# Fixed byte offsets for the moving operands of a decoder step: H at 96 and L at 0 modulo 256

## The chip, the cores and the metric

The kernel runs on one NeuronCore of one Trainium2 chip. The metric is the device time of one execution in microseconds (us), lower is better; several executions are timed and the median is quoted. A profile of one execution gives, for each engine, when each instruction began and how long it was busy. The engines are PE (matrix multiply, with PEld as its weight loads), DVE (elementwise, vector), ACT (activation functions), POOL (GpSimd) and SP (which only issues DMAs here).

## The reference, cut to what matters

One inference step of a two-layer hybrid decoder, for 256 prompt positions and 8 sampled positions (264 columns together), model width 2048, float32. Layer 0 is dilated sliding-window attention and layer 1 an S5 state-space layer with a gated output; each is followed by a gated MLP with a causal convolution of width 3.

```
for i in range(DEPTH):
    hp = rms_norm(xp, norm_g[i, 0])
    ...
    xp = xp + rms_norm(mp, norm_g[i, 1])
    hp = rms_norm(xp, norm_g[i, 2])
    fp, cp = conv_ffn(hp, c0_p, w_up[i], conv_w[i], conv_b[i], w_down[i])
    xp = xp + rms_norm(fp, norm_g[i, 3])
```

The work is almost all in eight dense products with float32 weights: `w_qkv`, `w_o`, `w_up`, `w_down` of layer 0, `w_in`, `w_glu`, `w_up`, `w_down` of layer 1.

## The kernel before, in words

Activations lie transposed: 128 channels on the partitions, the 264 positions along the free dimension. To reach float32 accuracy with the faster float32r matmul, each operand is split in two parts that are rounded in turn: a high part H (ACT writes it) and the rest L (DVE writes it). A product is then three matmuls into one PSUM tile: weights-H with activations-H (line 202), weights-H with activations-L (line 203), weights-L with activations-H (line 204). The activations are the moving operand (264 columns), the 128x128 weight block is the stationary one, loaded anew for every matmul.

`gemm` (line 180) walks an order of (k, m) pairs, k a block of 128 input channels and m one of 128 output channels. Each order begins with a group of 4 to 6 output blocks that are done together, k outermost (`order_grouped`, line 67): there one moving operand pair serves several products one after the other. After it, one output block at a time runs through all k: there each product has another operand pair. There are 6176 products, so 18528 of these matmuls. Of the products, 16x5 in `w_qkv`, 8x5 in `w_o`, 16x6 in each `w_up`, 16x4 in `w_in` and 16x5 in `w_glu` stand in the groups, 456 in all; the other 5720 run in the second form.

Weights stream from HBM in tiles of 512 KB by SP; `ensure` and `split` (lines 165 and 161) make their H and L parts, on ACT and DVE, in buffers of 4096 bytes per partition.

Each H, each L, each block of the residual stream and each block of a product's output is a tile of 1056 bytes per partition (264 floats) from the function `act` (line 155). Most come from the pool `acts` of 44 such buffers (line 1213); the pools `o`, `z`, `ga` and `gb` hold more of them for a stage. A pool's buffers lie behind one another, so successive buffers start 1056 = 4 x 256 + 32 bytes apart, and the start of a buffer modulo 256 takes all eight multiples of 32. Which buffer an H or an L gets is a matter of which is free. In the built program the 6176 H operands start at all eight of these offsets, between 198 and 1456 times each, and so do the L operands. All weight parts start at 64 modulo 256 (block columns are 512 bytes apart).

`residual` (line 339) makes, block by block, the sum of stream and normed output, its H and L for the next product (`operand`, line 327) and its store to DRAM. `reload` (line 314) brings the stream back by DMAs that POOL issues, into free `act` buffers, long before `residual` needs it. DMAs issued by POOL use a scratch area for their descriptors, 16 KB per partition by default. The tile framework orders each engine's instructions by its own scheduler and adds the waits.

Of the kernel before, what the change touches and what calls it, by code (L numbers as in the profile page):

```python
# [17 lines left out]
F32 = mybir.dt.float32  # L18
F32R = mybir.dt.float32r
# [7 lines left out]
P = 128  # L27
# [34 lines left out]
GS = 6  # L62
WARM = (6, 8, 9)
POOL_K = (2, 3, 8, 9, 13)


def order_grouped(mts, nk, first):
# [56 lines left out]
class Kern:  # L124
    def __init__(self, ctx, tc, I, O):
        self.ctx, self.tc, self.nc, self.I, self.O = ctx, tc, tc.nc, I, O
        self.n = 0
        self.tick = 0
        self.tasks = []
        self.side = iter(())  # L130
        self.loaded = []

    def nm(self, s):
        self.n += 1
# [17 lines left out]
    def tt(self, out, a, b, op):  # L152
        self.nc.vector.tensor_tensor(out, a, b, op=op)

    def act(self, pool, dt=F32):
        return pool.tile([P, NT], dt, tag="act", name=self.nm("act"))

    def small(self, tag, bufs=2):
        return self.sp.tile([P, NT], F32, tag=tag, name=self.nm(tag), bufs=bufs)
# [142 lines left out]
    def yevac(self, ys, gi):  # L302

        sq = [None, None]

        def f(m, ps):
            y = self.act(self.actp)
            self.squares(sq, ps[:, 0:NT])
            self.nc.vector.tensor_scalar(y, ps[:, 0:NT], self.gain(gi, m), None, op0=ALU.mult)
            ys[m] = y  # L310

        return f, sq

    def reload(self, src, wait):

        xs = []

        def load(k):
            x = self.act(self.actp)
            self.nc.gpsimd.dma_start(x, src[k])  # L320
            xs.append(x)

        for k in range(KD):
            self.later(wait + k // 2, lambda k=k: load(k))
        return xs

    def operand(self, x, gi, k):

        nc = self.nc
        g = self.gain(gi, k)  # L330
        hi, lo = self.act(self.actp, F32R), self.act(self.actp, F32R)
        nc.scalar.activation(hi, x, AF.Copy, scale=g)

        def low():
            nc.vector.scalar_tensor_tensor(lo, x, g, hi.bitcast(F32), op0=ALU.mult, op1=ALU.subtract)  # L335

        return hi, lo, low
# [50 lines left out]
    def consts(self):  # L388
        nc, I = self.nc, self.I
        cp = self.cp  # L390
        self.gn = cp.tile([P, 8 * KD], F32, name="gn")
        nc.scalar.dma_start(self.gn, I["gn"])
        self.ident = cp.tile([P, P], F32, name="ident")
        self.later(2, lambda: nc.gpsimd.dma_start(self.ident, I["ident"]))
        self.onesm = cp.tile([P, 1], F32, name="onesm")
        nc.vector.memset(self.onesm, -0.5 / D)
        self.epsm = cp.tile([P, 1], F32, name="epsm")
        nc.vector.memset(self.epsm, -0.5 * EPS / P)
        self.wm = cp.tile([P, P], F32, name="wm")
        nc.vector.memset(self.wm, 1.0)  # L400
        self.ident15 = cp.tile([TB, TB], F32, name="ident15")
        self.later(6, lambda: nc.scalar.activation(self.ident15, self.ident[0:TB, 0:TB], AF.Copy, scale=1.5))
        self.ones = cp.tile([P, NS], F32, name="ones")
        nc.vector.memset(self.ones, 1.0)
# [279 lines left out]
    def prompt_out(self, ap, st, h, os_):  # L684

        nc = self.nc
        po = self.ps()
        hi, lo = st["o", h] = (self.act(self.bigp, F32R), self.act(self.bigp, F32R))
        st["left", h], st["os"] = 2, os_
        ps = {}  # L690

        def tr(g):

            pt = self.ps()
            for c in range(3):
                nc.tensor.transpose(pt[:, c * P : (c + 1) * P], st["S", g, h][:, c * P : (c + 1) * P], self.ident)
            ps[g] = ap.tile([P, 384], F32, tag="pt", name=self.nm("pt"), bufs=3)
            nc.scalar.activation(ps[g], pt[:, 0:384], AF.Copy)

        def pv(g):  # L700
            vt, p = st["vt", g, h], ps[g]
            nc.tensor.matmul(po[:, 0:256], vt[:, 0:128], p[:, 0:256], start=(g == 0), stop=False)
            nc.tensor.matmul(po[:, 128:256], vt[:, 128:256], p[:, 256:384], start=False, stop=(g == G - 1))
            if g == G - 1:
                self.split(hi[:, 0:NP], lo[:, 0:NP], po[:, 0:NP])
                self.finished(st, h)

        for g in range(G):
            self.later(g, lambda g=g: tr(g))
            self.later(g + 1, lambda g=g: pv(g))  # L710
# [24 lines left out]
    def ffn(self, fp, l, rhs, rget, prep, gi, src, gpool):  # L735
        nc, I, O = self.nc, self.I, self.O
        cw, cst, keep = prep
        gate = {}
        gs = [None] * FT

        def evac(m, ps):
            u = fp.tile([P, NT], F32, tag="U", name=self.nm("U"), bufs=6)
            nc.vector.tensor_tensor(u, ps[:, 0:NT], rget(), op=ALU.mult)  # L743
            nc.gpsimd.tensor_copy(keep[:, m, :], u[:, NP - 2 : NT])  # L744
            c = fp.tile([P, NT], F32, tag="C", name=self.nm("C"), bufs=4)
            nc.scalar.activation(c, u, AF.Identity, bias=cw[:, 3, m : m + 1], scale=cw[:, 2, m : m + 1])  # L746
            self.later(1, lambda: conv(m, u, c))

        def conv(m, u, c):
            for j in (1, 0):  # L750
                s = 2 - j
                nc.vector.scalar_tensor_tensor(  # L752
                    c[:, s:NP], u[:, 0 : NP - s], cw[:, j, m : m + 1], c[:, s:NP], op0=ALU.mult, op1=ALU.add
                )
            nc.vector.tensor_tensor(c[:, NP:NT], c[:, NP:NT], cst[:, m, :], op=ALU.add)  # L755
            if m < FT:
                nc.scalar.activation(c, c, AF.Silu)  # L757
                gate[m] = c
            else:
                self.later(1, lambda: out(m - FT, c))  # L760

        def out(m, c):
            g = gate.pop(m)
            nc.vector.tensor_tensor(g, g, c, op=ALU.mult)  # L764
            hi, lo = self.act(gpool(m), F32R), self.act(gpool(m), F32R)
            nc.scalar.activation(hi, g, AF.Copy)  # L766
            gs[m] = (hi, lo)
            self.later(1, lambda: nc.vector.tensor_tensor(lo, g, hi.bitcast(F32), op=ALU.subtract))

        self.gemm("w_up%d" % l, ORD_UP, KD, rhs, evac, lag=3)  # L770
        xs = self.reload(src, 8)
        self.later(6, lambda: nc.gpsimd.dma_start(O["conv"][l], keep))
        ys = [None] * KD
        f, sq = self.yevac(ys, gi)

        def grhs(k):
            if k == FT - 1 and self.gwait:
                while gs[k] is None or any(True for t in self.tasks if t[0] <= self.tick + 1):
                    self.pump()
                self.gwait = False  # L780
            return self.ready(gs, k)

        self.gwait = True
        self.gemm("w_down%d" % l, ORD_DOWN, FT, grhs, f)
        return ys, xs, sq
# [260 lines left out]
    def s5(self, p, rhs, rget):  # L1046
# [119 lines left out]
        def back(j, up, y):  # L1166
            V.scalar_tensor_tensor(y, up[:, :, 0:YC], dsk[:, j : j + 1], y, op0=ALU.mult, op1=ALU.add)
            z = p.tile([P, NT], F32, tag="z", name=self.nm("z"), bufs=2)
            A.activation(z[:, 0:NP].rearrange("p (c s) -> p s c", s=T4), y[:, :, 8:YC], AF.Gelu_apprx_tanh)
            A.activation(z[:, NP:NT], y[:, 0, 0:8], AF.Gelu_apprx_tanh)  # L1170
            zp = self.bigp if j < 10 else self.actp
            hi, lo = self.act(zp, F32R), self.act(zp, F32R)
            self.split(hi, lo, z)
            zs[j] = (hi, lo)
            if j == KD - 1:
                Q.dma_start(O["ssms"], news)
                Q.dma_start(O["ssmp"], newp)
# [4 lines left out]
    def glu(self, p, zs, gi):  # L1182
# [5 lines left out]
        def evac(m, ps):  # L1188
# [3 lines left out]
            m -= KD  # L1192
            sg = p.tile([P, NT], F32, tag="gsg", name=self.nm("gsg"), bufs=2)
            nc.scalar.activation(sg, ps[:, 0:NT], AF.Sigmoid)
            y = self.act(self.actp)
            nc.vector.tensor_tensor(y, half.pop(m)[:, 0:NT], sg, op=ALU.mult)
            self.squares(sq, y)
            nc.scalar.activation(y, y, AF.Copy, scale=self.gain(gi, m))
# [6 lines left out]
    def run(self):  # L1205
# [4 lines left out]
        self.wp = ent(tc.tile_pool(name="w", bufs=3))  # L1210
        self.sp = ent(tc.tile_pool(name="small", bufs=2))
        self.psp = ent(tc.tile_pool(name="psum", bufs=8, space=PSUM))
        self.actp = ent(tc.tile_pool(name="acts", bufs=44))
        self.stream, self.bases = [], {}
        for n in ("w_qkv", "w_o", "w_up0", "w_down0", "w_in", "w_glu", "w_up1", "w_down1"):
            self.bases[n] = len(self.stream)
# [7 lines left out]
        def ffn_layer(l, rhs, rget, keep, nxt):  # L1224
            with ExitStack() as s:
                fp = pool(s, f"ffn{l}")
                ga = pool(s, f"ga{l}", 2 * GA)
                gb = []
                s2 = ExitStack()
                if l == 0:  # L1230
# [3 lines left out]
                def gpool(m):  # L1234
# [5 lines left out]
                    if not gb:  # L1240
                        for _ in self.side:
                            pass
                        s2.close()
                        gb.append(pool(s, f"gb{l}", 2 * (FT - GA - GS)))
                    return gb[0]

                prep = self.ffn_prep(fp, l)
# [2 lines left out]

        with ExitStack() as s:
            ap = pool(s, "att")
            self.bigp = pool(s, "o", 2 * H)
            rhs, rget = self.first(ap, I["x"])
            setup = self.s5_setup(ap)
            self.later(70, lambda: setattr(self, "side", setup))
# [8 lines left out]
        rhs, rget = ffn_layer(0, rhs, rget, xd[1], 4)  # L1265
        with ExitStack() as s:
            p = pool(s, "s5")
            self.bigp = pool(s, "z", 20)
            zs = self.s5(p, rhs, rget)
            xs = self.reload(xd[1], 8)  # L1270
            ys, sq = self.glu(p, zs, 5)
# [174 lines left out]
```

## Time and profile before

| what | value |
|---|---|
| median of 3 executions | 2534.36 us (2530.38 to 2537.7) |
| profiled execution: own time | 2533.61 us |
| its span, first to last instruction | 2531.8 us |
| PE busy, share of the span | 2465.2 us, 97% |
| DVE, ACT, POOL busy | 1788.3, 1208.4, 853.9 us |
| mean granted TensorE clock, as a share of full speed | 0.989 |
| DMA traffic | 512.12 MB, mean 202 GB/s |

How to read it: the profile lists matmuls with a start and a modelled end. Matmuls are pipelined, so the busy time of one (some 285 ns) covers its neighbours, and what a matmul costs is the distance from its start to the start of the next. The other engines' times are those of single instructions.

### The profile page before, as it was taken

Reading aid. Unit: us, or ns where it says so; the run is one execution under the profiler, and the core shown is the slowest. Engines: PE = TensorE matmul, PEld = TensorE weight load, DVE = VectorE, ACT = ScalarE, POOL = GpSimd, SP = SyncE. Lnnn points to the kernel's source line nnn. Section 1 sums busy time; section 2 is a strip of 40 time slices with the busy share of each in tenths; the row PEclk is TensorE's granted clock in tenths of the full one; section 3 lists DMA queues with packets and bytes.
Section 4 is the critical chain, followed back from the end, with each engine's and each line's share of the span. In section 5 each row is a group of like instructions: output and inputs, shape, how many; then the busy total and the mean of one; then the engine's idle time right before and its main releaser. Section 6 shows DMA issues by size and latency. Waiting matters only on the chain.

```text
span 2531.8 us, 52652 instructions
## 1 busy us (share of the span) xinstructions
PE 2465.2 (97%) x20998; PEld 2437.6 (96%) x20998; DVE 1788.3 (71%) x3002; ACT 1208.4 (48%) x1946; POOL 853.9 (34%) x1153
## 2 busy tenths in 40 slices
PE   8999999999999999999999988999999999999997
PEld 8999999999999999999998988999999999999997
DVE  6788998779888887764446877446877777764444
ACT  5465545556454554443334333444654454443332
POOL 6444448344999980001004564102100000011001
PEclk9999999999999999999999998999999999999998
DMA  7676666665666665565556777555655555566553
GB/s 276 219 258 227 210 221 222 217 222 182 222 214 221 224 211 184 183 205 197 182 183 213 236 233 217 188 183 176 196 179 181 182 180 180 183 205 199 181 182 118
DMA packets 186870, 512.12 MB, mean 202 GB/s; under 512 B 39280, under 2 KB 68992, under 8 KB 186368
## 3 DMA queue, kind: packets, MB, share of 16 engines
q1 hardware_dynamic: 141808, 457.89, 55.4%
q0 software_dynamic: 7968, 26.71, 3.2%
q10 hardware_dynamic: 36848, 24.16, 3.1%
q8 instruction: 164, 2.69, 0.4%
q14 instruction: 82, 0.67, 0.1%
HBM read 469.80 MB, written 38.88 MB: 201 GB/s over the span
## 4 chain that ended last, share of the span: by engine, by line
PE 73%; DVE 11%; issue 4%; DMA 4%; POOL 3%; ACT 3%; ACTq 1%; SPq 0%; DVEq 0%; POOLq 0%
PE ps L204 23%; PE ps L202 23%; PE ps L203 23%; DVE wlo L163 4%; DVE C L752 2%; ACT whi L162 2%; DMA yb<-y 1%; POOL z_room L920 1%; ACTq L953 1%; DMA y<-yb 1%; DVE act L367 1%; DMA ident<-in_ident 1%; DVE act L335 1%; DVE C L755 0%; DVE U L743 0%
## 5 line engine op out<-in xcount | busy, mean ns | idle before, releaser
L202 PE MATMUL ps<-act,whi 128*128 128x264 f32 x6176 | 1771.8, 288 | 10.7 <-ACT whi L162 7.5
L204 PE MATMUL ps<-act,wlo 128*128 128x264 f32 x6176 | 1762.0, 286 | 18.5 <-DVE wlo L163 18.1
L203 PE MATMUL ps<-act,whi 128*128 128x264 f32 x6176 | 1760.7, 285 | 10.0 <-DVE act L335 9.7
L163 DVE TENSOR_TENSOR wlo<-wraw,whi 128x1024 fp32r<-128x1024 f32 (+1 forms) x775 | 978.2, 1263 | 585.3 <-ACT whi L162 584.5
L162 ACT ACTIVATE whi<-wraw 128x1024 fp32r<-128x1024 f32 (+1 forms) x775 | 814.2, 1053 | 894.8 <-PE ps L203 670.5
L204 PEld LDWEIGHTS ps<-act,wlo 128*128 128x128 f32 x6176 | 1168.6, 189 | 23.5 <-DVE wlo L163 23.4
L203 PEld LDWEIGHTS ps<-act,whi 128*128 128x128 f32 x6176 | 1169.0, 189 | 13.7 <-DVE act L335 12.9
L202 PEld LDWEIGHTS ps<-act,whi 128*128 128x128 f32 x6176 | 1165.8, 189 | 16.4 <-ACT whi L162 8.0
L294 POOL TENSOR_TENSOR acc<-acc,sq 128x264 f32<-128x264 f32 x112 | 112.6, 1005 | 669.0 <-ACT sq L300 666.4
L744 POOL COPY ckeep<-U 128x10 f32<-128x10 f32 x172 | 44.8, 261 | 643.7 <-DVE U L743 642.6
L752 DVE SCALAR_TENSOR_TENSOR C<-U,cw,C 128x255 f32<-128x255 f32 (+1 forms) x344 | 197.4, 576 | 0.7 <-ACT C L746 0.7
L746 ACT ACTIVATE C<-U,cw 128x264 f32<-128x264 f32 x172 | 102.3, 597 | 34.8 <-DVE U L743 30.5
L743 DVE TENSOR_TENSOR U<-ps,rstd 128x264 f32<-128x264 f32 x172 | 73.0, 429 | 62.9 <-PE ps L204 62.8
L449 POOL TENSOR_TENSOR qkv<-qkv,cs 32x264 f32<-32x264 f32 x48 | 59.7, 1243 | 123.5 <-DVE sw L443 45.6
L121 POOL TENSOR_TENSOR z_e<-z_pa,z_pb 128x256 f32<-128x256 f32 x64 | 69.1, 1080 | 5.0
L617 ACT ACTIVATE vc<-vc,pk 128x128 f32<-128x128 f32 x192 | 59.5, 390 | 17.2 <-DMA pk<-pd 17.2
L121 POOL TENSOR_TENSOR z_pa<-z_bc,z_tab 128x256 f32<-128x256 f32 x64 | 62.9, 983 | 2.4
L766 ACT ACTIVATE act<-C 128x264 fp32r<-128x264 f32 x86 | 35.5, 413 | 58.7 <-DVE C L764 58.7
L757 ACT ACTIVATE C<-C 128x264 f32<-128x264 f32 x86 | 35.7, 415 | 48.1 <-DVE C L752 44.4
L121 POOL TENSOR_TENSOR z_pb<-z_bc,z_tab 128x256 f32<-128x256 f32 x64 | 56.6, 884 | 0.0
L450 POOL TENSOR_TENSOR sw<-sw,cs 32x264 f32<-32x264 f32 x48 | 51.6, 1075 | 0.0
L668 ACT ACTIVATE S<-S,nmg 128x128 f32<-128x128 f32 (+1 forms) x48 | 21.4, 447 | 61.2 <-DVE nmg L663 61.2
(215 smaller groups left out, 1771.9 us busy)
## 6 DMA issues: line engine op xcount, KB each, us to landing
wraw<-in_w_up SPq DMA_DIRECT2D x344, 512.0 KB, 3.5
wraw<-in_w_down SPq DMA_DIRECT2D x172, 512.0 KB, 3.8
wraw<-in_w_qkv SPq DMA_DIRECT2D x143, 512.0 KB, 4.8
wraw<-in_w_glu SPq DMA_DIRECT2D x64, 512.0 KB, 3.5
wraw<-in_w_in SPq DMA_DIRECT2D x32, 512.0 KB, 3.9
kc<-in_kc SPq DMA_DIRECT2D x24, 512.0 KB, 5.4
vc<-in_vc SPq DMA_DIRECT2D x24, 512.0 KB, 5.9
wraw<-in_w_o SPq DMA_DIRECT2D x16, 512.0 KB, 3.6
```

The costliest lines, as they stand in the source:

```text
L121: return lambda *a, **k: self.tc.keep_in_program_order(getattr(self.eng, name)(*a, **k))
L162: self.nc.scalar.activation(hi, src, AF.Copy)
L163: self.nc.vector.tensor_tensor(lo, src, hi.bitcast(F32), op=ALU.subtract)
L202: nc.tensor.matmul(o, hi[:, c], xh, start=first, stop=False)
L203: nc.tensor.matmul(o, hi[:, c], xl, start=False, stop=False)
L204: nc.tensor.matmul(o, lo[:, c], xh, start=False, stop=last)
L294: nc.gpsimd.tensor_tensor(st[0], st[0], st[1], op=ALU.add)
L449: nc.gpsimd.tensor_tensor(t[0:ROT, :], t[0:ROT, :], self.cs[:, 0, :], op=ALU.mult)
L617: nc.scalar.activation(vcs[g][:, e], vcs[g][:, e], AF.Copy, scale=pk[:, g, e : e + 1])
L743: nc.vector.tensor_tensor(u, ps[:, 0:NT], rget(), op=ALU.mult)
L746: nc.scalar.activation(c, u, AF.Identity, bias=cw[:, 3, m : m + 1], scale=cw[:, 2, m : m + 1])
L752: nc.vector.scalar_tensor_tensor(c[:, s:NP], u[:, 0 : NP - s], cw[:, j, m : m + 1], c[:, s:NP], op0=ALU.mult, op1=ALU.add)
```

## The change

H and L of one operand now share one buffer, a slot of 576 floats = 2304 = 9 x 256 bytes: `pair` returns H at float 280 (1120 bytes, 96 modulo 256) and L at float 0. The pool `acts` has 22 slots in place of 44 buffers, the pools `o`, `ga`, `gb`, `z` half their number. Blocks that are no moving operand go in twos: `share(k)` puts the stream's block k and the output's block k in the two halves of one slot, at bytes 0 and 1152. Small pads in front (`pad`, with a memset of one element each) bring every pool's base to a multiple of 256. The scratch for POOL's DMAs is cut from 16 to 4 KB per partition.

In the built program every H then starts at 96 and every L at 0 modulo 256; and since the pad of the constants' pool lies ahead of the weight buffers, the weight parts move from 64 to 128 modulo 256. Number and shape of matmuls, weight loads and DMAs stay as they are.

```
+SLOT = 576
+HI, LO = 280, 0
...
-    def act(self, pool, dt=F32):
-        return pool.tile([P, NT], dt, tag="act", name=self.nm("act"))
+    def two(self, pool, dt=F32):
+        t = pool.tile([P, SLOT], dt, tag="act", name=self.nm("act"))
+        return t[:, 0:NT], t[:, SLOT // 2 : SLOT // 2 + NT]
+    def share(self, k):
+        if k in self.halves:
+            return self.halves.pop(k)
+        t, self.halves[k] = self.two(self.actp)
+        return t
+    def pair(self, pool):
+        t = pool.tile([P, SLOT], F32R, tag="act", name=self.nm("act"))
+        return t[:, HI : HI + NT], t[:, LO : LO + NT]
+    def pad(self, pool, n):
+        t = pool.tile([P, n], F32, tag="pad", name=self.nm("pad"), bufs=1)
+        self.tc.keep_in_program_order(self.nc.vector.memset(t[:, 0:1], 0.0))
...
-            y = self.act(self.actp)
+            y = self.share(m)
...
-            x = self.act(self.actp)
+            x = self.share(k)
...
-        hi, lo = self.act(self.actp, F32R), self.act(self.actp, F32R)
+        hi, lo = self.pair(self.actp)
...
+        self.pad(cp, 16)
...
-        self.actp = ent(tc.tile_pool(name="acts", bufs=44))
+        self.actp = ent(tc.tile_pool(name="acts", bufs=22))
...
+                self.pad(fp, 8)
+                ga = pool(s, f"ga{l}", GA)
...
-    nc = bacc.Bacc("TRN2", target_bir_lowering=False, num_devices=1)
+    nc = bacc.Bacc("TRN2", target_bir_lowering=False, num_devices=1, dynamic_dma_scratch_size=4096)
```

The change in the slots also moves some instructions. On PE, at the start of the product with `w_up` of layer 0, stood before (`act_7667` is the H of block 0, `act_7668` its L, the six `ps` are the first six output blocks):

```order
L202 MATMUL ps_7698<-act_7667,whi_7519 128x264
L202 MATMUL ps_7702<-act_7667,whi_7519 128x264
L202 MATMUL ps_7706<-act_7667,whi_7519 128x264
L202 MATMUL ps_7710<-act_7667,whi_7519 128x264
L202 MATMUL ps_7714<-act_7667,whi_7519 128x264
L202 MATMUL ps_7718<-act_7667,whi_7519 128x264
L226 MATMUL ps_8161<-epsm,wm 88x1
L203 MATMUL ps_7698<-act_7668,whi_7519 128x264
L204 MATMUL ps_7698<-act_7667,wlo_7520 128x264
L203 MATMUL ps_7702<-act_7668,whi_7519 128x264
```

and now (`act_7633` holds both parts):

```order
L226 MATMUL ps_7661<-act_7633,whi_7485 128x264
L226 MATMUL ps_7665<-act_7633,whi_7485 128x264
L226 MATMUL ps_7669<-act_7633,whi_7485 128x264
L226 MATMUL ps_7673<-act_7633,whi_7485 128x264
L227 MATMUL ps_7661<-act_7633,whi_7485 128x264
L228 MATMUL ps_7661<-act_7633,wlo_7486 128x264
L227 MATMUL ps_7665<-act_7633,whi_7485 128x264
L228 MATMUL ps_7665<-act_7633,wlo_7486 128x264
```

Lines 226, 227, 228 of the changed file are lines 202, 203, 204 of the one before (line 226 of the one before is a one-column matmul of the norm). Four products with H stand ahead of the first with L, where there were six.

On POOL, near the end of the product with `w_qkv`, where the residual stream is brought back for the first sum, stood before:

```order
L600 COPY vn_6939<-qkv_6688 128x8
L320 DMA act_7141<-in_x 128x264
L600 COPY vn_6939<-qkv_6788 128x8
L320 DMA act_7143<-in_x 128x264
L320 DMA act_7148<-in_x 128x264
L320 DMA act_7150<-in_x 128x264
L600 COPY vn_6939<-qkv_6878 128x8
```

and now:

```order
L625 COPY vn_6920<-qkv_6669 128x8
L625 COPY vn_6920<-qkv_6769 128x8
L344 DMA act_7026<-in_x 128x264
L344 DMA act_7028<-in_x 128x264
L344 DMA act_7076<-in_x 128x264
L344 DMA act_7078<-in_x 128x264
L344 DMA act_7112<-in_x 128x264
L344 DMA act_7114<-in_x 128x264
L344 DMA act_7121<-in_x 128x264
L344 DMA act_7123<-in_x 128x264
L344 DMA act_7128<-in_x 128x264
L344 DMA act_7130<-in_x 128x264
L625 COPY vn_6920<-qkv_6859 128x8
```

Ten of the sixteen loads now wait for the end of that product, where four did; the other six stand at its beginning, as twelve did.

## Rows read from the trace of the kernel before

**Rows 1.** The page's first part: busy time, share of the span, instructions.
```profile
span 2531.8 us, 52652 instructions
PE 2465.2 (97%) x20998; PEld 2437.6 (96%) x20998; DVE 1788.3 (71%) x3002; ACT 1208.4 (48%) x1946; POOL 853.9 (34%) x1153
```

**Rows 2.** The page's groups: line engine op out<-in xcount | busy, mean ns | idle before, releaser.
```profile
L202 PE MATMUL ps<-act,whi 128*128 128x264 f32 x6176 | 1771.8, 288 | 10.7 <-ACT whi L162 7.5
L204 PE MATMUL ps<-act,wlo 128*128 128x264 f32 x6176 | 1762.0, 286 | 18.5 <-DVE wlo L163 18.1
L203 PE MATMUL ps<-act,whi 128*128 128x264 f32 x6176 | 1760.7, 285 | 10.0 <-DVE act L335 9.7
```

**Rows 3.** Three stretches: length, busy (count) of PE, PEld, DVE, ACT, POOL; clock; DMA.
```profile
1100.00:1350.00 250.00, 250.00 (x2063) 250.00 (x2062) 117.45 (x117) 98.39 (x107) 25.23 (x38) 1.00 0.59 192
1820.00:2240.00 420.00, 420.00 (x3454) 420.00 (x3453) 300.97 (x505) 210.76 (x288) 13.81 (x72) 1.00 0.57 181
2300.00:2500.00 200.00, 200.00 (x1658) 200.00 (x1657) 90.24 (x82) 77.45 (x82) 13.74 (x13) 1.00 0.56 183
```

**Rows 4.** Timeline of PE: first matmul of successive runs on one operand pair (start, us).
```profile
19.89 0.28 PE L202 MATMUL ps<-act,whi 128*128 128x264 f32 x1
...
21.71 0.28 PE L202 MATMUL ps<-act,whi 128*128 128x264 f32 x1
...
23.54 0.28 PE L202 MATMUL ps<-act,whi 128*128 128x264 f32 x1
...
25.35 0.29 PE L202 MATMUL ps<-act,whi 128*128 128x264 f32 x1
...
1770.62 0.28 PE L202 MATMUL ps<-act,whi 128*128 128x264 f32 x1
...
1772.78 0.28 PE L202 MATMUL ps<-act,whi 128*128 128x264 f32 x1
...
1774.99 0.29 PE L202 MATMUL ps<-act,whi 128*128 128x264 f32 x1
...
1780.34 0.28 PE L202 MATMUL ps<-act,whi 128*128 128x264 f32 x1
...
1782.52 0.28 PE L202 MATMUL ps<-act,whi 128*128 128x264 f32 x1
```

**Rows 5.** Timeline of PE: the same two products in two successive passes over k.
```profile
2003.04 0.28 PE L202 MATMUL ps<-act,whi 128*128 128x264 f32 x1
...
2003.40 0.29 PE L202 MATMUL ps<-act,whi 128*128 128x264 f32 x1
...
2008.88 0.28 PE L202 MATMUL ps<-act,whi 128*128 128x264 f32 x1
...
2009.24 0.29 PE L202 MATMUL ps<-act,whi 128*128 128x264 f32 x1
```

**Rows 6.** Timeline of PE: the start of the product with w_up of layer 0.
```profile
566.17 0.97 PE L202 MATMUL ps<-act,whi 128*128 128x264 f32 x6
566.97 0.24 PE L226 MATMUL ps<-epsm,wm 128*88 128x1 f32 x2
567.34 0.39 PE L203 MATMUL ps<-act,whi 128*128 128x264 f32 x1
```

**Rows 7.** Timeline of POOL at the end of w_qkv: idle before, in us, and its releaser.
```profile
502.75 0.58 POOL L320 DMA_DIRECT2D act<-in_x  x1 [7.09 <-PE ps L204]
...
508.93 0.19 POOL L600 COPY vn<-qkv 128x8 f32<-128x8 f32 x1 [3.87 <-DVE qkv L437]
```

**Rows 8.** The reloads by tile: duration ns min/median/max, first and last start; then landing.
```profile
L320 POOL DMA_DIRECT2D act<-in_x x16: 536/536/582, 36.6 to 504.5; - x16
...
DMA to landing us min/median/max: 2.4/5.2/8.0
```

**Rows 9.** A memset of one element per partition on DVE (same columns).
```profile
L396 DVE MEMSET onesm<- x1: 59/59/59, 0.8 to 0.8; 128x1 f32 x1
```

More of the change, by code (lines that the diff above doesn't have):

```diff
@@ L131, in __init__ @@
         self.loaded = []
+        self.halves = {}
     def nm(self, s):
@@ L687, in prompt_out @@
         po = self.ps()
-        hi, lo = st["o", h] = (self.act(self.bigp, F32R), self.act(self.bigp, F32R))
+        hi, lo = st["o", h] = self.pair(self.bigp)
         st["left", h], st["os"] = 2, os_
@@ L764, in out @@
             nc.vector.tensor_tensor(g, g, c, op=ALU.mult)
-            hi, lo = self.act(gpool(m), F32R), self.act(gpool(m), F32R)
+            hi, lo = self.pair(gpool(m))
             nc.scalar.activation(hi, g, AF.Copy)
@@ L1171, in back @@
             zp = self.bigp if j < 10 else self.actp
-            hi, lo = self.act(zp, F32R), self.act(zp, F32R)
+            hi, lo = self.pair(zp)
             self.split(hi, lo, z)
@@ L1194, in evac @@
             nc.scalar.activation(sg, ps[:, 0:NT], AF.Sigmoid)
-            y = self.act(self.actp)
+            y = self.share(m)
             nc.vector.tensor_tensor(y, half.pop(m)[:, 0:NT], sg, op=ALU.mult)
@@ L1226, in ffn_layer @@
                 fp = pool(s, f"ffn{l}")
-                ga = pool(s, f"ga{l}", 2 * GA)
+                self.pad(fp, 8)
+                ga = pool(s, f"ga{l}", GA)
                 gb = []
@@ L1243, in gpool @@
                         s2.close()
-                        gb.append(pool(s, f"gb{l}", 2 * (FT - GA - GS)))
+                        gb.append(pool(s, f"gb{l}", FT - GA - GS))
                     return gb[0]
@@ L1252, in run @@
             ap = pool(s, "att")
-            self.bigp = pool(s, "o", 2 * H)
+            self.pad(ap, 24)
+            self.bigp = pool(s, "o", H)
             rhs, rget = self.first(ap, I["x"])
@@ L1267, in run @@
             p = pool(s, "s5")
-            self.bigp = pool(s, "z", 20)
+            self.pad(p, 56)
+            self.bigp = pool(s, "z", 10)
             zs = self.s5(p, rhs, rget)
```

## The prediction, made before the changed kernel was run

> **What bounds the kernel.** I read the first part of the page first: PE is busy 97% of the span, and no other engine over 71% [rows 1]. Then the costliest groups: three lines of matmul, 6176 each, 18528 together, and the engine stood idle ahead of them for only 10.7, 18.5 and 10.0 us [rows 2]. So hardly any time is lost to waiting, and the kernel can become faster only where the matmuls themselves follow each other faster. Busy time does not show that, because each matmul is listed with some 285 ns while the next one starts long before. I therefore took stretches in which PE does nothing but these matmuls and divided length by count: 250/2063, 420/3454 and 200/1658, that is 121.2, 121.6 and 120.6 ns from start to start; together 870 us for 7175, or 121.3 ns. [...]
>
> [...] In the groups at the head of a product the same H and L serve 5 or 6 products, 15 or 18 matmuls. From 1770.62 to 1772.78 run 18 on a pair whose H and L both start at 192 modulo 256 (all addresses here are those of the built program): 2.16 us, 120.0 ns each. The next 18, to 1774.99, have H at 224 and L at 32: 2.21 us, 122.8 ns [rows 4]. Shape, engine and clock are the same, and no idle time is marked; only the buffers differ. The order of 2% is what is at stake: 2% of 18528 x 121.3 ns is 45 us.
>
> [...]
>
> **The change, part by part.**
>
> *Offsets.* Every triple of matmuls will read H at 96, L at 0, H at 96 modulo 256. The trace before has this pair, in two settings.
> First, as a run: 19.89 to 21.71, 15 matmuls in 1.82 us, and 1780.34 to 1782.52, 18 in 2.18 us [rows 4]; together 33 in 4.00 us, 121.2 ns. This is the exact sequence that the changed kernel will run all the time, but seen for a few repeats, in the head groups, where DVE and ACT are also making the next operands.
> Second, as one product in the passes over k: 2003.04 to 2003.40, and a pass later 2008.88 to 2009.24, each 0.36 us for three matmuls, 120.0 ns [rows 5]. This is the setting of 5720 of the 6176 products, but with other pairs before and behind.
> By the first the term is (121.2 - 121.3) x 18528 = -2 us; by the second (120.0 - 121.3) x 18528 = -24 us. I take -24, since it comes from the form in which 93% of the products run, and keep -2 as the upper end of this case. The fastest run that I read, at 1770.62, has the same 120.0 [rows 4]; but a sequence that repeats without change for 2 ms may settle lower (the last rival).
>
> *Weights.* They move from 64 to 128 modulo 256. No row shows weights at another offset, so what it costs must be bounded. If the weights' place means nothing, 0. If only the distance between operand and weights counts, the changed kernel (H 32 below the weights, L 128 from them) is what the trace shows for weights at 64, H at 32 and L at 192: the run from 21.71 to 23.54, 15 matmuls in 1.83 us, 122.0 ns [rows 4], so +0.7 x 18528 = +13 us against 121.3. I take 0 for the sum, and +13 is the rival.
>
> *Order at the start of a product.* Before, six products with H covered the wait for the first L: PE ran them from 566.17, and the first matmul with L came at 567.34 [rows 6]. Now four do. The two that stand behind L are done later, so at most 2 x 0.12 us is lost at such a start; the order changed at the start of four products, the first of them `w_qkv`, where five covered and one is left (4 x 0.12 us). That makes 3 x 0.24 + 0.48 = 1.2 us at most; I take 1 us.
>
> *Slots held by two.* Ten loads of the stream instead of four wait for the slots of `w_qkv`, and they stand in POOL's queue ahead of the copy for the last head, which must not come late. Ten at 0.54 us [rows 8] from 502.75 take until 508.2; the copy waited for DVE until 508.93 anyway [rows 7]. Hidden, with 0.7 us to spare. They land up to 8.0 us after issue [rows 8], so by 517; the sum that reads them leads straight into the product that starts at 566 [rows 6]. Cost 0. In `residual` a new pair needs a slot whose two halves are both done with; six slots are free at its start, so block k waits for the store of block k - 6. Blocks follow each other at the pace of 18 matmuls, 2.2 us [rows 4], so six take 13 us, and a store would have to take that long to be felt. 0.
>
> *Scratch of 4 KB.* No row shows a lack of descriptors. The reloads, POOL's commonest transfers, land in 2.4 to 8.0 us [rows 8]. Bounds: 0, or the landing of one of them, 8 us, once, if POOL had to wait at the start when its loads come thickest. I take 0. *Pads:* five memsets of 59 ns [rows 9], on an engine that is idle 29% of the time [rows 1]: 0.
>
> *Sum.* The profiled execution took 2533.6 us, 0.8 below the median of the three. 2533.6 - 24 + 1 = 2510.6, say **2511 us**.
>
> **Rivals.**
>
> *Slower: the distance to the weights decides.* PE and its weight loads are busy side by side, 2465 and 2438 us of 2532 [rows 1]: a matmul reads its columns while the next weights are read. If the two reads get in each other's way, only their distance can matter, and the 64 bytes that the weights move undo what the operands' new places gave. For it: runs with the same distance between L and H (160) do not take the same time, 121.3 for 96 and 0 against 122.0 for 32 and 192, and 1.81 us for 15, 120.7, for 224 and 128 (23.54 to 25.35) [rows 4]; so something fixed is the other partner, and the weights are the one that stood still. Against: no row shows it with moved weights. Price +13, with the +1 above: 2533.6 + 14 = 2548 us. It is slower beyond the measurement (below) once the mean gap passes 121.3 + 7.6/18.528 = 121.7 ns. Chance 0.26.
>
> *No effect.* The gaps shown are 10 ns steps over few matmuls; in a long stream differences of 1 to 2 ns may be absorbed by whatever else limits PE (the weight load, as long as a matmul), or the exact run's 121.2 is the truth. Price 0 to -2, plus 1: 2533 to 2535 us. Chance 0.15.
>
> *Much faster.* All 18528 now run in one repeating pattern. If it settles as far below 120.0 as 120.0 lies below the mean, at 118.7 (an estimate), that is -2.6 x 18528 = -48 us: 2486 us. For it: the run at 1770.62 is the one where H and L have one offset and everything repeats, and it is the fastest read [rows 4]. Against: 96 and 0 gave 121.2 when repeated. Chance 0.12.
>
> *My forecast*, the pair behaves as in the passes, with its spread from -2 to -24 and a little below: 0.47.
>
> **How the numbers follow.** A measurement of this kernel tells 0.3%, 7.6 us, from no change; so faster means below 2526.8. My forecast's case lies there but for its upper end (0.04 of its 0.47 goes to "same"), and so does the fourth: faster 0.55. Same: the no-effect case and that end, 0.19. Slower: 0.26. The likeliest case's own range is 2500 to 2533. The range for 8 in 10 takes in the slower rival with 2 us of the small costs on top, 2550, and reaches down to 2475 for most of the fourth case.
>
> **What would show it.** In the profile of the changed kernel the three pure stretches should hold more matmuls: at 120.0 ns, 3500 where 3454 stood in 420 us. Counts below 3454 mean the weights' distance. All three stretches should now have one gap, since the 121.2, 121.6 and 120.6 of before came from different mixes of offsets. PE's idle time ahead of the three lines should stay within 2 us of what it was; POOL's copy at 508.9 should still wait for DVE. The forecast is wrong in its reason if the time falls while the gaps stay, and wrong in size if the gap is not between 119.9 and 121.2 ns.

## The result and the profile after

The changed kernel is slower: 2549.61 us, median of 5 runs (2548.41 to 2557.93), against 2534.36; ratio 1.0072, 95% interval 1.005 to 1.0094. The forecast was 2511. The time is that of the rival "the distance to the weights decides" (2548). The execution profiled was the slowest of the five, 2557.93 us, 24.3 us more than the one profiled before.

The first part of the page and the three costliest groups of the changed kernel; lines 226, 227, 228 are the old 202, 203, 204 [rows 1, 2]:

```profile
span 2556.1 us, 52679 instructions
...
PE 2482.1 (97%) x20998; PEld 2453.2 (96%) x20998; DVE 1799.0 (70%) x3007; ACT 1209.8 (47%) x1946; POOL 863.0 (34%) x1153
...
L226 PE MATMUL ps<-act,whi 128*128 128x264 f32 x6176 | 1782.9, 290 | 14.1 <-ACT whi L186 8.7
L228 PE MATMUL ps<-act,wlo 128*128 128x264 f32 x6176 | 1759.8, 285 | 15.6 <-DVE wlo L187 15.3
L227 PE MATMUL ps<-act,whi 128*128 128x264 f32 x6176 | 1766.0, 286 | 8.2 <-DVE act L359 8.1
```

The idle time ahead of the three lines is 37.9 us in all, where it was 39.2: no wait ahead of them took the time. (Over the whole span PE is idle for 74.0 us, where it was 66.6; the difference lies ahead of other matmuls and is counted below in "rest".) The same three stretches as in [rows 3], of the changed kernel (window, its length, then busy time and count of PE, PEld, DVE, ACT, POOL, the granted clock, DMA share, GB/s):

```profile
1100.00:1350.00 250.00, 250.00 (x2011) 250.00 (x2010) 116.68 (x120) 96.96 (x107) 24.38 (x34) 1.00 0.58 188
1820.00:2240.00 420.00, 420.00 (x3439) 420.00 (x3438) 305.35 (x523) 213.96 (x296) 16.41 (x74) 1.00 0.55 180
2300.00:2500.00 200.00, 200.00 (x1639) 200.00 (x1638) 89.64 (x82) 76.04 (x80) 12.23 (x12) 1.00 0.55 181
```

2011, 3439 and 1639 matmuls stand where 2063, 3454 and 1658 stood: 124.3, 122.1 and 122.0 ns from start to start, at the same clock. Most of the time went into the gap between matmuls. But the three stretches differ, though all addresses are now alike modulo 256.

In what follows, "gap" is the mean distance from one of these matmuls to the next, over all neighbouring records of the trace under 140 ns, and "rest" is the span less 18528 gaps: stops, other matmuls, stretches at a granted clock of 0.50 (in the kernel before, for one, from 1583.8 to 1586.0 us, with gaps of 220 ns), start and end. Before: gap 121.54, rest 279.9 us. Changed: gap 122.63, rest 284.0. So 1.09 x 18528 = 20.2 of the 24.3 us are gaps. The rest is that of one execution each, and another profile of the changed kernel, further down, has 279.0.

A clue lay in the gaps themselves. In most of its stages the changed kernel repeats six gaps, 120, 122, 121, 121, 125, 124 ns (mean 122.2); the kernel before had the same six in the run from 21.71 to 23.54 [rows 4], where H at 32, L at 192 and weights at 64 have the same distances as now 96, 0 and 128. In the first `w_down` it repeats three others, 124, 123, 126 (124.4).

### The profile page after: what moved, and what is told of

Read it like the earlier page. It is cut to its first block, busy times and chain, and to the rows that moved or that the text cites. A ratio compares the mean times of both kernels' runs of the same rounds, so it can differ in the third digit from the quotient of the medians.

```text
span 2556.1 us, 52679 instructions
## 1 busy us (share of the span) xinstructions
PE 2482.1 (97%) x20998; PEld 2453.2 (96%) x20998; DVE 1799.0 (70%) x3007; ACT 1209.8 (47%) x1946; POOL 863.0 (34%) x1153
## 4 chain that ended last, share of the span: by engine, by line
PE 73%; DVE 9%; POOL 7%; DMA 5%; issue 3%; ACT 3%; ACTq 0%; SPq 0%; DVEq 0%; POOLq 0%
PE ps L226 23%; PE ps L227 23%; PE ps L228 23%; DVE wlo L187 3%; DMA yb<-y 2%; POOL z_pb L125 1%; ACT whi L186 1%; POOL z_room L945 1%; POOL z_pa L125 1%; POOL z_e L125 1%; DVE act L359 1%; POOL z_wt L125 1%; DVE z_room L945 1%; DMA ub<-up 1%; DMA y<-yb 1%
## 5 line engine op out<-in xcount | busy, mean ns | idle before, releaser
L768 DVE TENSOR_TENSOR U<-ps,rstd 128x264 f32<-128x264 f32 x172 | 73.1, 429 | 72.4 <-PE ps L228 69.6
L476 POOL TENSOR_TENSOR qkv<-qkv,sw 32x264 f32<-32x264 f32 x48 | 49.2, 1025 | 3.4
```

## The experiments

A pair (a, b) below means: H starts a bytes and L starts b bytes above the weights, modulo 256. The changed kernel is (224, 128). Theory D says that this pair sets the gap; theory A that the offsets of H and L by themselves do; theory O that slots, order or scratch cost the time.

**The gap by itself, for all pairs.** The model is replaced by 128 cells of 14 triples each:

```
for wo in MAPW:
    for h in range(8):
        for l in range(8):
            ...
            for r in range(REP):
                ...
                xh, xl = hb[:, 8 * h : 8 * h + NT], lb[:, 8 * l : 8 * l + NT]
                pin(nc.tensor.matmul(o, wh[:, c], xh, start=(r == 0), stop=False))
                pin(nc.tensor.matmul(o, wh[:, c], xl, start=False, stop=False))
                pin(nc.tensor.matmul(o, wl[:, c], xh, start=False, stop=(r == REP - 1)))
```

H starts at 160 + 32 h, L at 160 + 32 l, the weights first at 160, then at 224 modulo 256.

Expected:

> This kernel computes nothing of the model (it only copies one input to one output); it measures the gap by itself. 8 by 8 offsets of H and L modulo 256, in steps of 32, with 14 triples of H, L, H each (42 matmuls of 264 columns in one tile), first with both weights at 160, then with both at 224 modulo 256. Theory D (the distances of H and of L from the weights set the gap): the table of the second half is that of the first, moved by two steps in H and in L; the cell of distances (-32, -128) shows some 122 ns, (+32, -64) some 121.0, (160, 64) 120.0. Theory A (the offsets of H and L by themselves): the second table equals the first, cell by cell, unmoved. Theory O (the rest of the change cost the time): all cells within 1 ns of each other.

Measured, mean of the last 18 gaps of a cell in ns, by distance (down: H minus weights, 0 to 224 in steps of 32; across: L minus weights), first with the weights at 160:

```
        0    32    64    96   128   160   192   224
  0     -  120.0 121.2 121.4 122.1 122.4 121.1 120.7
 32  122.2 122.2 120.8 121.4 120.0 121.1 121.1 122.2
 64  122.2 121.9 120.9 121.1 121.4 120.0 121.5 121.5
 96  122.2 122.2 122.9 122.0 121.7 121.8 120.0 122.2
128  122.2 122.2 122.2 123.3 120.0 122.2 122.2 122.9
160  122.2 122.2 120.0 122.2 122.2 121.7 122.2 123.3
192  121.8 122.2 121.5 122.2 121.1 122.2 120.0 120.7
224  122.2 121.5 122.2 122.2 122.2 122.2 120.0 120.0
```

(The first cell fell into the start, where gaps of 220 ns still stand; with the weights at 224 it shows 120.0.) With the weights at 224, so all cells moved by two steps in H and in L, 56 of the 63 cells differ by 0.2 ns or less from this table; compared by the offsets of H and L alone, 17 do. One cell in the timeline of PE: the starts of two matmuls 30 gaps apart, for (160, 224) with weights at 160; then, with weights at 224, for the same H and L; then for the same distances.

```profile
250.90 0.29 PE L1236 MATMUL ps<-hb,wh 128*128 128x264 f32 x1
...
254.60 0.29 PE L1236 MATMUL ps<-hb,wh 128*128 128x264 f32 x1
...
577.59 0.28 PE L1236 MATMUL ps<-hb,wh 128*128 128x264 f32 x1
...
581.25 0.28 PE L1236 MATMUL ps<-hb,wh 128*128 128x264 f32 x1
...
628.87 0.29 PE L1236 MATMUL ps<-hb,wh 128*128 128x264 f32 x1
...
632.57 0.29 PE L1236 MATMUL ps<-hb,wh 128*128 128x264 f32 x1
```

3.70, 3.66 and 3.70 us: 123.3, 122.0 and 123.3 ns. The gap goes with the distances. Two more things are in the table: no cell is below 120.0, and its mean is 121.6, about the gap of the kernel before with its mixed offsets (121.5). The other seven cells differ between the halves by up to 1.5 ns; why, a later experiment shows in part.

**The weights put back.** The pad of 16 floats now behind the weight buffers, so that they start at 64 again:

```
-        self.pad(cp, 16)
...
+        self.pad(ent(tc.tile_pool(name="gap", bufs=1)), 16)
```

> The changed kernel with the 64 bytes that had moved the weights put behind them: weights start at 64 modulo 256 again, H 96, L 0 as in the changed kernel. Theory D: distances are those of the kernel before's run of 18 with H at 96 and L at 0, whose gap was 121.0 to 121.2 ns, against 122.2 to 122.6 in the changed kernel: -1.2 to -1.6 ns x 18528 = -22 to -30 us, so 2520 to 2527 us. Theory A: H and L have not moved, so nothing changes: 2548 to 2555 us. Theory O: 2548 to 2555 us as well.

Measured: 2535.78 us, ratio to the kernel before 1.0014 (1.0004 to 1.0024); gap 121.14, rest 289.7 us.

**All three moved.** `HI, LO = 296, 16`:

> The changed kernel with H at 160 and L at 64 modulo 256 and the weights left at 128: all three lie 64 bytes above where they lie in the run with the weights put back, so all distances are the same as there. Theory D: the same time as that run, 2520 to 2527 us, and the same sequence of gaps. Theory A: H and L at 160 and 64 gave about 122 ns in the kernel before, so 2540 to 2550 us. Theory O: 2548 to 2555 us.

Measured: 2537.41 us, ratio 1.0016 (1.0005 to 1.0027); gap 121.15, rest 291.0 us. The longest stretch in both, (32, 192) at two places in memory, the weights put back first:

```profile
1820.00:2240.00 420.00, 420.00 (x3471) 420.00 (x3469) 304.09 (x511) 212.23 (x291) 15.71 (x73) 1.00 0.57 182
```

```profile
1820.00:2240.00 420.00, 420.00 (x3470) 420.00 (x3469) 304.65 (x513) 212.42 (x291) 16.78 (x73) 1.00 0.56 182
```

3471 and 3470 matmuls where the changed kernel has 3439. The gap is the map's 121.1 in both, though no operand lies at the same offset: D stands, A falls, and O falls as what made the changed kernel slower. But both times missed the 2520 to 2527 of D, by some 10 us. Against the kernel before the gap gave 0.40 x 18528 = 7.4 us, and the rest took 10 back, more than was won: both ratios lie just above 1. So a few us of O, in slots or order, are not excluded.

**Another pair.** `HI, LO = 8, 304`, so (160, 64):

> The changed kernel with H at 32 and L at 192 modulo 256 and the weights left at 128: distances 160 and 64, those of the kernel before's run with H at 224 and L at 128 beside weights at 64, whose gap was 120.0 to 120.7 ns. Theory D: 120.0 to 120.7 instead of 122.4 ns: -1.7 to -2.4 ns x 18528 = -31 to -44 us, so 2505 to 2518 us. Theory A: H at 32 and L at 192 gave 122.0 ns in the kernel before: -0.4 ns x 18528 = -7 us, so 2541 to 2548 us. Theory O: 2548 to 2555 us.

Measured: 2522.17 us, ratio 0.9964 (0.9953 to 0.9975); gap 120.27, rest 292.4 us. The gap is as D has it, but the time missed the 2505 to 2518: of the 23.5 us that the gap gave against the kernel before, the rest took 12.5 back.

**The scratch alone**, in the kernel before:

```
-    nc = bacc.Bacc("TRN2", target_bir_lowering=False, num_devices=1)
+    nc = bacc.Bacc("TRN2", target_bir_lowering=False, num_devices=1, dynamic_dma_scratch_size=4096)
```

> The kernel before with the scratch cut to 4 KB and nothing else; every buffer moves down by 12 KB, a multiple of 256, so all offsets modulo 256 stay. Theory D (distances decide): no change, 2531 to 2536 us. Theory O, in what is left of it (the stops between the matmuls grew from 254 us in the kernel before to 264 us in the run with the weights put back): if the scratch makes those, 2538 to 2543 us.

Measured: 2532.78 us, ratio 0.9999 (0.9989 to 1.0008); gap 121.54, rest 277.7. It costs nothing that shows.

**Two candidates and the worst pair.** `HI, LO = 304, 8`, (64, 160); `32, 296`, (0, 32); `8, 280`, (160, 224):

> The changed kernel with H at 192 and L at 32 modulo 256, weights left at 128: distances 64 and 160, where the map shows 120.0 ns in both halves and from the first repeats on (the mean of all 41 gaps is 119.9 there, against 120.8 for 160 and 64, which needs some 20 matmuls to settle). Theory D: 120.0 to 120.1 instead of the 120.27 of the run with 160 and 64: -3 to -5 us against its 2522, so 2517 to 2519 us. Rival G (what the gaps still give goes into waits for weights' L parts and for the round trips through DRAM, which do not end earlier): 2521 to 2524 us. Theory A: no expectation below 2535.

> The changed kernel with H at 128 and L at 160 modulo 256, weights left at 128: distances 0 and 32, 120.0 and 119.9 ns in the map once settled, but in one half only after some 25 matmuls (mean of all 41 gaps 120.0 and 120.6). Theory D: 120.0 to 120.6, so 2517 to 2528 us, and within 6 us of the run with 64 and 160. If a matmul whose columns start where the weights start were bad in itself, as one would think of a conflict between the two reads, this would be the slowest of all: above 2560 us.

> The changed kernel with H at 32 and L at 96 modulo 256, weights left at 128: distances 160 and 224, the slowest cell of the map, 123.2 ns in both halves. Theory D: 123.2 - 120.27 = 2.9 ns x 18528 = 54 us more than the run with 160 and 64, so 2570 to 2577 us, less what longer gaps take out of the stops (up to 10 us): 2560 to 2577, slower than the changed kernel. Theory A: H has not moved from the run at 2522 us, and L at 96 has no bad place of its own known; 2522 to 2550 us.

Measured, in the same order: 2525.7 us, ratio 0.9966 (0.9953 to 0.9979), gap 120.84, rest 288.1; 2527.51 us, 0.9973 (0.996 to 0.9986), gap 120.44, rest 298.7; 2560.81 us, 1.0103 (1.0089 to 1.0117), gap 123.13, rest 280.6. The worst pair is slower than the changed kernel, as D says. Equal starts of columns and weights, (0, 32), are no conflict in themselves. The first candidate missed both its ranges: the windows of (64, 160) show why, and those of (0, 32), which stand behind them, show the same more weakly.

```profile
1100.00:1350.00 250.00, 250.00 (x2048) 250.00 (x2047) 116.39 (x117) 97.68 (x106) 24.22 (x33) 1.00 0.56 191
1820.00:2240.00 420.00, 420.00 (x3502) 420.00 (x3501) 306.44 (x515) 214.03 (x294) 14.97 (x74) 1.00 0.55 184
```

```profile
1100.00:1350.00 250.00, 250.00 (x2067) 250.00 (x2066) 118.75 (x122) 98.98 (x109) 24.46 (x34) 1.00 0.57 192
1820.00:2240.00 420.00, 420.00 (x3502) 420.00 (x3502) 307.13 (x518) 214.47 (x294) 16.57 (x74) 1.00 0.56 184
```

For (64, 160), 250/2048 is 122.1 ns in the first `w_down`, 420/3502 is 119.9 later: one pair, two gaps, as in the changed kernel. For (0, 32) 250/2067 is 120.9, and the single gaps there have a mean of 121.1, against 120.0 later. That asked for the next experiment.

**Many starts of the same pair.** Nine pairs, ten starts each of 22 triples, ahead of each start one matmul of another width:

```
+REP = 22
+TRIES = 10
+CELLS = [(7, 4), (1, 6), (5, 2), (2, 5), (0, 1), (5, 7), (3, 6), (1, 4), (4, 4)]
...
+        for n in range(TRIES):
+            for h, l in CELLS[n % len(CELLS) :] + CELLS[: n % len(CELLS)]:
...
+                pin(nc.tensor.matmul(ps[:, 0 : 32 + 16 * n], wh[:, 0:P], hb[:, 0 : 32 + 16 * n], start=True, stop=True))
```

> This kernel computes nothing of the model either. Nine pairs of distances (H minus weights, L minus weights), each started ten times anew behind one matmul of another width (32 to 176 columns), 66 matmuls per start. Theory P (a pair of distances has more than one steady cycle, and the start decides which): 64 and 160 settles at 120.0 in some starts and at 122.2 in others, -32 and -128 (the changed kernel's) at 122.2 and at 124.4 at least once; 160 and 64 and 32 and -64 always at one gap (120.0 and 121.1), as they did in the kernels. Rival Q (one cycle per pair, and what differed in the kernels was other traffic: DMA, ACT, DVE): every start of a pair settles at one gap.

Measured, ns once settled: (224, 128) 122.2 in 8 starts and 124.4 in 2; (64, 160) 120.0 in 7 and 124.4 in 3; (128, 128) 120.0 in 6 and 123.3 in 4; (160, 224) 123.3 in 9 and 122.8 in 1; and at one value in all ten: (32, 192) 121.1, (160, 64), (0, 32), (96, 192) and (32, 128) 120.0. Two starts of (224, 128) in the timeline of PE, each by two matmuls 48 gaps apart:

```profile
214.85 0.28 PE L1237 MATMUL ps<-hb,wh 128*128 128x264 f32 x1
...
220.72 0.28 PE L1237 MATMUL ps<-hb,wh 128*128 128x264 f32 x1
...
279.90 0.29 PE L1237 MATMUL ps<-hb,wh 128*128 128x264 f32 x1
...
285.88 0.29 PE L1237 MATMUL ps<-hb,wh 128*128 128x264 f32 x1
```

5.87 and 5.98 us: 122.3 and 124.6 ns, the two gaps of the changed kernel, with the same sequences of single gaps as there. DVE, ACT and POOL were busy for 0.00 us meanwhile, so for these pairs P holds and Q falls: a pair can have two steady cycles, and the start decides. But two pairs do not fit what the first `w_down` showed: (64, 160) had 122.2 ns there, and here 120.0 or 124.4; (0, 32) had 121.1 there, and here 120.0 in all ten starts. What else in the full kernel decides there, other traffic or the addresses beyond 256, was not tested.

**The changed kernel profiled again**, with no edit:

> The changed kernel itself, for another profile. Theory P: its runs lie between about 2548 and 2558 us, and a profile with a time T shows matmuls in the first w_down either at 122.2 ns (T near 2548) or at 124.4 ns (T near 2553 or more; 2.2 ns x 2064 is 4.5 us for that product alone). Rival Q: the first w_down always shows 124.4 ns, 2011 matmuls in 250 us.

Measured: 2547.51 us, ratio 1.0071 (1.005 to 1.0092); the execution profiled took 2545.28.

```profile
1100.00:1350.00 250.00, 250.00 (x2047) 250.00 (x2047) 116.54 (x117) 97.53 (x106) 24.54 (x34) 1.00 0.58 190
1820.00:2240.00 420.00, 420.00 (x3439) 420.00 (x3438) 301.96 (x511) 211.01 (x289) 15.51 (x72) 1.00 0.56 180
```

2047 in the first `w_down` where the first execution had 2011, and the same 3439 later. Gap 122.22, rest 279.0: against the kernel before, 0.68 x 18528 = +12.6 us of gaps and -0.9 of rest make the 11.7 us between the two spans. One of its six runs took 2562.76; why that one was slower, no trace shows.

**Two pairs that settled at 120.0 in every start.** `HI, LO = 296, 0`, (32, 128), and `312, 16`, (96, 192):

> The changed kernel with H at 160 and L at 0 modulo 256, weights left at 128: distances 32 and 128, one of the four pairs that settled at 120.0 ns in all ten starts. Against the changed kernel only H moves, by 64 bytes. Theory D with P: 120.0 to 120.4 ns on the mean, 420 us hold 3495 to 3502 matmuls, all runs within 10 us of each other, 2518 to 2526 us, as the run with 160 and 64 (2522). If other traffic can push a pair off the cycle that it has in the map, 250 us of the first w_down hold under 2080 and the time is 2525 to 2533 us.

> The changed kernel with H at 224 and L at 64 modulo 256, weights left at 128: distances 96 and 192, which settled at 120.0 ns in all ten starts, every gap 120 without a cycle, but after up to 24 matmuls at 121 to 122. Theory D with P: 2519 to 2528 us, gap 120.0 in the long products and some 0.5 more in the first ones, where stops are frequent. The same other outcome as for 32 and 128: 2525 to 2533 us.

Measured: 2522.43 us, ratio 0.9958 (0.9944 to 0.9973), gap 120.18, rest 290.6; and 2522.22 us, 0.9958 (0.9944 to 0.9972), gap 120.31, rest 299.9. Both beat the kernel before and the changed one. The windows of (32, 128), which differs from the changed kernel by 64 bytes in H alone:

```profile
1100.00:1350.00 250.00, 250.00 (x2085) 250.00 (x2085) 117.81 (x117) 99.30 (x107) 26.16 (x37) 1.00 0.60 196
1820.00:2240.00 420.00, 420.00 (x3502) 420.00 (x3502) 304.77 (x510) 214.05 (x292) 14.00 (x73) 1.00 0.56 183
2300.00:2500.00 200.00, 200.00 (x1676) 200.00 (x1676) 87.47 (x81) 74.42 (x79) 12.34 (x12) 1.00 0.52 168
```

119.9, 119.9 and 119.3 ns: here the stretches have one gap (the last 3 us of the third lie behind the last product, among shorter matmuls). Against the kernel before: 1.36 x 18528 = 25.2 us won in the gaps, 10.7 lost in the rest, 14.5 in the span; by the medians (2522.43 against 2533.43 beside it) 11.0.

**Where the rest differs** is shown in two places. The groups of PE from 840 to 960 us, of (96, 192), profiled at 2530.82 us, and of (32, 128), at 2519.12; L972 belongs to the preparation of the state-space layer, which runs beside the product:

```profile
L972 PE MATMUL ps<-ident,z_wt 128*128 128x128 f32 x20 | 3.2, 283 | 6.5 <-POOL z_wt L125 6.5
```

```profile
L972 PE MATMUL ps<-ident,z_wt 128*128 128x128 f32 x20 | 3.0, 272 | 0.0
```

In the one PE waits 6.5 us for POOL, in the other not at all; the first profile of the changed kernel, with its long gaps, has 4.3 us of it from 800 to 1000. So this wait goes with the execution, and it is not shown to go with the gap. The second place does: near the start of `w_glu` PE stands until an operand has been to DRAM and back, first in the kernel before (7.15 us out, 2.36 back), then with (160, 64) (6.74 out, 3.98 back):

```profile
1582.81 0.39 PE L202 MATMUL ps<-act,whi 128*128 128x264 f32 x1 [3.19 <-ACT act L162]
```

```profile
1580.56 0.59 PE L226 MATMUL ps<-act,whi 128*128 128x264 f32 x1 [4.63 <-ACT act L186]
```

With (160, 64) PE was there 3.7 us earlier (its last matmul started at 1575.65, against 1579.33), the operand 2.3 us earlier. That is 1.4 us of the 3.7 taken back. How the 10 us or so divide over all such places is open, and so is what in the chip makes the map; neither was tried. PE's idle time over the whole span does not answer it: 66.6 us before, 72.4 with (32, 128), 76.2 with (160, 64), but also 74.3 with (160, 224), the slowest pair.

## Why the prediction was wrong

*What bounds the kernel, and that the gap depends on where the operands lie: right.* The clock stayed at 1.00 in the three stretches, the waits ahead of the three lines at what they were, and moving H, L or weights alone moved the gap between 120.2 and 123.1 ns.

Two terms of the sum failed, and the runs price both. With the weights back the time was 2535.78, some 25 us above the forecast's 2511: that is *Offsets*, which gave 7.4 us in the gaps and not 24, and what the rest took back. Moving the weights took the time on to 2549.61, another 14 us: that is *Weights*. The rival's +13 was taken against the mean of 121.3, so it stands in place of both terms: with it the sum is 2548.

*Weights, "I take 0": the step that failed first.* Where the weights lie does count: the distances set the gap (with H and L at 96 and 0, 121.14 ns beside weights at 64, 122.63 and 122.22 beside weights at 128). The price of the other bound was right: +13 us from the run at the same distances, and the second profile shows +12.6 in the gaps. There is some luck in that: the run was read at 122.0, where the kernel settles at 122.2, and the mean of the three stretches, 121.3, lies as much below the kernel's 121.5. What decided against it was only that no row showed moved weights. But [rows 4] held an argument that I gave to the rival and not to the sum: pairs with one distance between L and H had different gaps, so something fixed had to be the partner.

*Offsets, -24: wrong too, even had the weights stayed.* With H at 96, L at 0 and weights at 64 the gap is 121.1, as the repeated run said (121.2, [rows 4]), and not the 120.0 of single products in the passes [rows 5]. There the neighbours were other pairs; the changed kernel repeats one. I chose the row by how many products run in that place, where the sequence that is repeated should have chosen. By the first reading the term would have been -2; the run with the weights back, gap and all, came out some 3 us above the kernel before (ratio 1.0014), with its gaps 7.4 us shorter.

*A gap counted 18528 times: wrong for gains.* No step asked what else limits the pace. With gaps of 120.2 to 121.2 the rest of the span is 288 to 300 us, with 121.5 and more 278 to 284; the two highest, (0, 32) and (96, 192), come from executions 4.5 and 8.6 us above the median of their runs. Of 25.2 us won in the gaps with (32, 128) 14.5 reach the end of the profiled execution, 11.0 by the medians. Losses count about in full: the second profile's +12.6 became 11.7, and the 29.5 of the worst pair became 30.2 in the span. That the shorter gap itself makes the rest longer is argued; no run shows it alone.

*Small costs: right for the scratch, not settled for the others.* The scratch costs nothing that shows (ratio 0.9999). In the second profile the rest is 279.0 against 279.9, so there slots, pads and order together cost nothing that shows; but no run tests them singly, and with the weights back the rest took more than the gaps gave. POOL's ten loads ended at 509.63 (506.88 + 2.75) and its copy started at 509.85, after 0.22 us of waiting for DVE: hidden, with hardly anything to spare. The last loads and the copy, in the first profile:

```profile
506.88 2.75 POOL L344 DMA_DIRECT2D act<-in_x  x5 [0.20 <-PE ps L228]
509.85 0.19 POOL L625 COPY vn<-qkv 128x8 f32<-128x8 f32 x1 [0.22 <-DVE qkv L462]
```

*The rivals.* "No effect" does not hold: with shape, clock and engine equal the map has gaps of 120.0 to 123.3 ns. The rival's "the weight load, as long as a matmul" was a misreading: both engines are busy almost all the span, but one weight load is listed with 189 ns and one matmul with 285 to 288 (page of the kernel before). "Much faster" (118.7) is excluded for the 64 pairs in steps of 32 bytes: none settles below 120.0. The sign named for the rival, counts below 3454 in 420 us, came as written (3439). "All three stretches now have one gap" did not: they had 124.3, 122.1 and 122.0 ns, and a pair can have two cycles.

## What to carry to other kernels

For matmuls of this form (264 columns, a fresh weight load each, no stop between them), the start of moving operand and weights modulo 256, taken as a difference, is worth some 3% of the gap (120.0 to 123.3 ns in the map); other forms were not measured. Before fixing addresses, measure all pairs in a kernel of their own, each with several starts, take a pair that settles at the lowest gap of the map (120.0 ns here) every time, and look at it in the full kernel as well: (0, 32) passed the ten starts and still had 121.1 ns in one product. Fixing the addresses is no gain in itself: the mixed kernel here had about the mean of the table (121.5 against 121.6 ns), a fixed one has one cell of it. And read the precursor of a repeated sequence from a place where it is repeated.

## What the runs showed of the hardware

The gap of 264-column matmuls with weight loads between them never settled below 120.0 ns at a granted clock of 1.00, at any of 64 pairs of distances, and with H, L and weights at given distances modulo 256 it settles, mostly within some 24 matmuls, to a fixed cycle of single gaps of 115 to 133 ns. Some pairs have two such cycles, up to 4.4 ns apart (120.0 and 124.4 for (64, 160)), and keep the one they fell into until the next stop: the first profile of the changed kernel holds 124.4 ns from 950 to 1370 us (3377 matmuls). One and the same program showed its first `w_down` at 122.1 ns in one execution and at 124.3 in another, each time with the sequence of one of the two cycles that its pair has in the kernel of starts. In the kernel before, one plain float32 product of 256 columns (line 648, two records at 491.59 us) held PE for 0.43 us, one float32r matmul of 264 columns for 0.12.
